# Rotary embedding, interleaved: how the last three batch rows leave the chip

## The chip, the cores and the metric

The kernel runs on one core of one Trainium2 chip. The metric is the device time of one execution in microseconds. A profile of one execution, taken by the hardware profiler, stands beside the times; its times count from the start of its span.

## What is computed

The input `x` has shape (8, 2048, 16, 64) in fp32: batch, sequence position, head, head dimension. Neighbouring elements of the head dimension form pairs, and each pair is rotated by an angle that depends on the position and the pair; `cos` and `sin` have shape (2048, 32).

```python
x_pairs = x.reshape(batch, seq_len, num_heads, head_dim // 2, 2)
x1 = x_pairs[..., 0]
x2 = x_pairs[..., 1]
out1 = x1 * cos - x2 * sin
out2 = x1 * sin + x2 * cos
out = np.stack([out1, out2], axis=-1).reshape(batch, seq_len, num_heads, head_dim)
```

The output has the shape and the type of `x`. So 67.1 MB are read and 67.1 MB written in HBM, and each element takes three arithmetic operations.

## The kernel before

The 2048 positions are laid over 128 partitions with K = 16 positions each. One batch row (called a row below) is thus a tile of 128 partitions by 16 x 1024 elements, 8.39 MB in fp32. In SBUF a row is held in bf16. The tile `xt` has NX = 5 places for rows, and the list `HOME` gives each row its place: rows 5, 6 and 7 use the places of rows 0, 1 and 2 again.

The conversion between fp32 in HBM and bf16 in SBUF is done by the DMA itself. Such a casting DMA is issued by GpSimd: `load(b, n)` and `store(b, n)` (lines 61 to 67) move n rows each with one DMA, and all of them are in one queue, GpSimd's. There are two exceptions, at the two ends of the kernel. The first four positions of row 0 (HEAD) come in as fp32 by a DMA that SyncE issues, into the tile `st`, and ScalarE casts them (line 101). The last four positions of row 7 (TAIL) go out by the same way backwards: ScalarE casts them to fp32 (line 132), and SyncE issues the DMA (line 133).

`rotate(b)` (lines 69 to 88) is three VectorE instructions over a row: a product with the sine table into the scratch tile `qt`, a product with the cosine table in place, and a sum in place that reads `qt` with the two elements of each pair exchanged.

The order is written out by hand, under a manual schedule. GpSimd works its instructions off in that order; each waits for the semaphores of what it needs. The loads of rows 0 to 4 are all issued at the start. Behind them GpSimd's order is:

```python
store(0, 1)
store(1, 2)                 # behind rotate(2)
load(5, 1)
load(6, 2)
store(3, 2)                 # behind rotate(4)
store(5, 2)                 # behind rotate(6)
# line 127: row 7 without its last four positions, behind rotate(7)
```

Then the tail follows. Line 131 is a ScalarE copy of one element into the place of row 6, and so it waits for the store of rows 5 and 6 to have landed. The cast of line 132 and the DMA of line 133 stand behind it.

The kernel ends with a closing sequence, which the profile puts on line 159: SyncE waits for the DMAs, each engine drains, and the engines meet by semaphores.

Of the kernel before, what the change touches and what calls it, by code (L numbers as in the profile page):

```python
# [2 lines left out]

# [4 lines left out]


@with_exitstack  # L10
def kernel(
    ctx: ExitStack,
    tc: tile.TileContext,
    x: bass.AP,
    cos: bass.AP,
    sin: bass.AP,
    out: bass.AP,
):
    nc = tc.nc
    fp32 = mybir.dt.float32  # L20
    bf16 = mybir.dt.bfloat16
    mult = mybir.AluOpType.mult
    add = mybir.AluOpType.add

    B, S, H, D = x.shape
    P = 128
    K = S // P
    KP = 16
    D2 = D // 2
    HD = H * D  # L30
    NX = 5
    HEAD = 4
    TAIL = 4
    LAST = 2


    HOME = [0, 1, 2, 3, 4, 0, 1, 2]

    x_t = x.rearrange("b (p k) h d -> b p k (h d)", p=P, k=K)
    out_t = out.rearrange("b (p k) h d -> b p k (h d)", p=P, k=K)  # L40
    x_r = x.rearrange("b (p k) h d -> p b (k h d)", p=P, k=K)
    out_r = out.rearrange("b (p k) h d -> p b (k h d)", p=P, k=K)
    cos_t = cos.rearrange("(p k) c -> p (k c)", p=P, k=K)
    sin_t = sin.rearrange("(p k) c -> p (k c)", p=P, k=K)

    consts = ctx.enter_context(tc.tile_pool(name="consts", bufs=1))
    stage = ctx.enter_context(tc.tile_pool(name="stage", bufs=1))

    xt = consts.tile([P, NX, K * HD], bf16)
    cos_sb = consts.tile([P, K * D2], fp32)  # L50
    sin_sb = consts.tile([P, K * D2], fp32)
    c_tab = consts.tile([P, K, D], bf16)
    s_tab = consts.tile([P, K, D], bf16)

    gate = consts.tile([1, 1], bf16)
    mark = consts.tile([1, 1], bf16)

    def home(b, k0=0, k1=K):
        return xt[:, HOME[b], k0 * HD : k1 * HD].rearrange("p (k c) -> p k c", c=HD)

    def load(b, n):
        h = HOME[b]
        nc.gpsimd.dma_start(out=xt[:, h : h + n], in_=x_r[:, b : b + n])  # L63

    def store(b, n):
        h = HOME[b]
        nc.gpsimd.dma_start(out=out_r[:, b : b + n], in_=xt[:, h : h + n])  # L67

    def rotate(b, k0=0, k1=K):
        nk = k1 - k0  # L70
        xp = home(b, k0, k1)
        qt = stage.tile([P, KP, HD], bf16, name="qt", tag="work")

        def rows(a):
            return a.rearrange("p k (h e) -> p k h e", h=H, e=D)

        def tab(a):
            return dataclasses.replace(
                a, offset=a.offset + k0 * D, ap=[a.ap[0], [D, nk], [0, H], [1, D]]
            )  # L80

        nc.vector.tensor_tensor(out=rows(qt[:, :nk]), in0=rows(xp), in1=tab(s_tab), op=mult)  # L82
        nc.vector.tensor_tensor(out=rows(xp), in0=rows(xp), in1=tab(c_tab), op=mult)  # L83
        q_swap = dataclasses.replace(
            qt, offset=qt.offset + 1, ap=[qt.ap[0], [2, nk * HD // 2], [-1, 2]]
        )
        x3 = xp.rearrange("p k (a j) -> p (k a) j", j=2)
        nc.vector.tensor_tensor(out=x3, in0=x3, in1=q_swap, op=add)  # L88

    with tc.manual_schedule():  # L90
        head = stage.tile([P, TAIL, HD], fp32, name="st", tag="work")
        nc.sync.dma_start(out=head[:, :HEAD], in_=x_t[0, :, :HEAD])
        nc.gpsimd.dma_start(out=home(0, HEAD), in_=x_t[0, :, HEAD:])  # L93
        nc.gpsimd.dma_start(out=cos_sb, in_=cos_t)  # L94
        nc.gpsimd.dma_start(out=sin_sb, in_=sin_t)  # L95
        load(1, 2)
        load(3, 1)
        nc.gpsimd.dma_start(out=home(4, 0, K - LAST), in_=x_t[4, :, : K - LAST])  # L98
        nc.gpsimd.dma_start(out=home(4, K - LAST), in_=x_t[4, :, K - LAST :])  # L99

        nc.scalar.copy(out=home(0, 0, HEAD), in_=head[:, :HEAD])  # L101
        s2 = s_tab.rearrange("p k (i j) -> p (k i) j", j=2)
        nc.vector.tensor_copy(out=s2[:, :, 0], in_=sin_sb)  # L103
        nc.vector.tensor_scalar_mul(s2[:, :, 1], sin_sb, -1.0)  # L104
        nc.vector.tensor_copy(  # L105
            out=c_tab.rearrange("p k (i j) -> p (k i) j", j=2),
            in_=cos_sb.to_broadcast([P, K * D2, 2]),
        )
        rotate(0, 0, HEAD)
        rotate(0, HEAD, K)  # L110
        nc.scalar.copy(out=gate, in_=home(4, K - LAST - 1, K - LAST)[:1, 0, :1])  # L111
        nc.scalar.copy(out=xt[:1, HOME[0], :1], in_=xt[:1, HOME[0], :1])  # L112
        store(0, 1)
        rotate(1)
        rotate(2)
        nc.gpsimd.tensor_copy(out=mark, in_=xt[:1, 4, K * HD - 1 :])  # L116
        store(1, 2)
        load(5, 1)
        load(6, 2)
        rotate(3)  # L120
        rotate(4)
        store(3, 2)
        for b in range(5, B):
            rotate(b)
            if b == 6:
                store(5, 2)
        nc.gpsimd.dma_start(out=out_t[B - 1, :, : K - TAIL], in_=home(B - 1, 0, K - TAIL))  # L127

        tail = stage.tile([P, TAIL, HD], fp32, name="st", tag="work")
        last = home(B - 1, K - TAIL, K)  # L130
        nc.scalar.copy(out=xt[:1, HOME[B - 2], :1], in_=xt[:1, HOME[B - 1], K * HD - 1 :])  # L131
        nc.scalar.copy(out=tail, in_=last)  # L132
        nc.sync.dma_start(out=out_t[B - 1, :, K - TAIL :], in_=tail)


# [1 line left out]
_INS = ['x', 'cos', 'sin']  # L137
_OUTS = [((8, 2048, 16, 64), 'float32')]


# [23 lines left out]
```

## Time and profile before

| what | value |
|---|---|
| median of 3 runs | 316.26 us (316.24 to 316.33) |
| span of the profiled execution | 314.4 us; the profile gives no total of its own for it, so the runs stand beside it, 1.8 to 1.9 us above |
| VectorE busy | 210.4 us (67%) |
| ScalarE busy | 8.9 us (3%) |
| GpSimd busy | 13.9 us (4%) |
| GpSimd's DMA queue | 98.04 MB, 96.8% of 16 engines |
| SyncE's DMA queue | 4.19 MB, 3.3% of 16 engines |
| HBM | 67.63 MB read, 67.11 MB written |

DVE is VectorE, ACT ScalarE, POOL GpSimd, SP SyncE; a "q" behind the name is the engine's queue or sequencer. An instruction that issues a DMA is not counted as busy time of the transfer: it is done after half a microsecond or so, while the data move much later. For each DMA issue the profile gives the time to its landing, which is when the completion of the whole transfer has been signalled. The size in KB that stands beside some issues is that of the destination.

### The profile page before, as it was taken

To read this page: it belongs to the slowest core of one execution; us is meant where nothing else is said; L and a number is where in the kernel's file an instruction comes from. 1 tells how busy PE (TensorE), PEld (TensorE's weight loads), DVE (VectorE), ACT (ScalarE), POOL (GpSimd) and SP (SyncE) were. 2 spreads that over 40 slices of the span, in tenths; PEclk is the share of its full clock that TensorE was granted. 3 is DMA by queue.
4 is the path that set the end of the run, shared out by engine and by line. 5 is a ranking of instruction groups with operands and counts; after the bars stand their busy time and mean duration, and the time that the engine had idled before them with its cause. 6 is when DMAs were issued, how large, how long until landed. Compare 5 with 4: busy or idle time off the path is not lost.

```text
span 314.4 us, 116 instructions
## 1 busy us (share of the span) xinstructions
DVE 210.4 (67%) x30; ACT 8.9 (3%) x6; POOL 13.9 (4%) x19
## 2 busy tenths in 40 slices
DVE  0009995099999999999992399903999999200000
ACT  1040000000000000000000000000000000000400
POOL 5000000000002400000000000000000000000000
DMA  7999999999999999999999999999999999999997
GB/s 254 263 283 200 200 200 267 200 200 213 229 233 258 425 509 400 400 459 475 400 200 246 221 200 200 254 213 333 400 525 409 400 400 525 409 400 400 434 434 333
DMA packets 2816, 102.24 MB, mean 325 GB/s; under 512 B 256, under 2 KB 256, under 8 KB 512
## 3 DMA queue, kind: packets, MB, share of 16 engines
q0 software_dynamic: 2528, 98.04, 96.8%
q1 hardware_dynamic: 288, 4.19, 3.3%
HBM read 67.63 MB, written 67.11 MB: 429 GB/s over the span
## 4 chain that ended last, share of the span: by engine, by line
another core or an unknown queue 87%; DMA 5%; ACT 1%; ACTq 1%; issue 0%
DMA st<-in_x_dram 5%; ACT xt L101 1%; ACTq L159 1%; ACT xt L131 0%; ACT xt L112 0%; ACTq L131 0%; ACT gate L111 0%
## 5 line engine op out<-in xcount | busy, mean ns | idle before, releaser
L82 DVE TENSOR_TENSOR qt<-xt,s_tab 128x16384 bf16<-128x16384 bf16 (+2 forms) x9 | 69.7, 7743 | 34.4 <-DMA xt<-in_x_dram 34.3
L83 DVE TENSOR_TENSOR xt<-xt,c_tab 128x16384 bf16<-128x16384 bf16 (+2 forms) x9 | 69.7, 7744 | 0.4
L88 DVE TENSOR_TENSOR xt<-xt,qt 128x16384 bf16<-128x16384 bf16 (+2 forms) x9 | 69.7, 7744 | 0.3
L103 DVE CAST s_tab<-sin_sb 128x512 bf16<-128x512 f32 x1 | 0.5, 458 | 23.8 <-DMA sin_sb<-in_sin_dram 23.8
L67 POOL DMA_DIRECT2D out_dram<-xt x4 | 2.7, 671 | 185.5 <-ACT xt L112 93.8
L131 ACT COPY xt<-xt 1x1 bf16<-1x1 bf16 x1 | 0.2, 193 | 195.4 <-DMA out_dram<-xt 195.4
L116 POOL COPY mark<-xt 1x1 bf16<-1x1 bf16 x1 | 5.0, 5014 | 1.4 <-DMA xt<-in_x_dram 1.4
L63 POOL DMA_DIRECT2D xt<-in_x_dram x4 | 2.6, 656 | 43.0 <-DMA out_dram<-xt 43.0
L101 ACT CAST xt<-st 128x4096 bf16<-128x4096 f32 x1 | 3.6, 3604 | 13.3 <-DMA st<-in_x_dram 13.3
L132 ACT CAST st<-xt 128x4096 f32<-128x4096 bf16 x1 | 3.6, 3598 | 0.0
L111 ACT COPY gate<-xt 1x1 bf16<-1x1 bf16 x1 | 0.2, 193 | 79.7 <-DMA xt<-in_x_dram 79.7
L127 POOL DMA_DIRECT2D out_dram<-xt x1 | 0.6, 572 | 25.5 <-DVE xt L88 25.5
L101 ACT ACT_TABLE_LOAD x1 | 1.3, 1283 | 0.7 <-PEq L148 0.7
L93 POOL DMA_DIRECT2D xt<-in_x_dram x1 | 0.7, 680 | 0.8 <-PEq L159 0.8
L105 DVE CAST c_tab<-cos_sb 128x1024 bf16<-128x1024 f32 x1 | 0.7, 684 | 0.0
L99 POOL DMA_DIRECT2D xt<-in_x_dram x1 | 0.6, 592 | 0.0
L98 POOL DMA_DIRECT2D xt<-in_x_dram x1 | 0.6, 586 | 0.0
L95 POOL DMA_DIRECT2D sin_sb<-in_sin_dram x1 | 0.6, 562 | 0.0
L94 POOL DMA_DIRECT2D cos_sb<-in_cos_dram x1 | 0.6, 554 | 0.0
L104 DVE TENSOR_SCALAR s_tab<-sin_sb 128x512 bf16<-128x512 f32 x1 | 0.4, 445 | 0.0
L112 ACT COPY xt<-xt 1x1 bf16<-1x1 bf16 x1 | 0.2, 189 | 0.0
L148 POOL MEMSET const-float32-0.0<- 128x1 f32 x1 | 0.1, 93 | 0.2 <-issue 0.2
(3 smaller groups left out, 0.3 us busy)
## 6 DMA issues: line engine op xcount, KB each, us to landing
xt<-in_x_dram POOLq DMA_DIRECT2D x2, 8192.0 KB, 58.5
xt<-in_x_dram POOLq DMA_DIRECT2D x2, 4096.0 KB, 67.6
out_dram<-xt POOLq DMA_DIRECT2D x1, 6144.0 KB, 40.9
xt<-in_x_dram POOLq DMA_DIRECT2D x1, 3584.0 KB, 94.3
xt<-in_x_dram POOLq DMA_DIRECT2D x1, 3072.0 KB, 21.2
st<-in_x_dram SPq DMA_DIRECT2D x1, 2048.0 KB, 14.5
out_dram<-st SPq DMA_DIRECT2D x1, 2048.0 KB, 15.5
xt<-in_x_dram POOLq DMA_DIRECT2D x1, 512.0 KB, 96.3
```

The costliest lines, as they stand in the source:

```text
L63: nc.gpsimd.dma_start(out=xt[:, h : h + n], in_=x_r[:, b : b + n])
L67: nc.gpsimd.dma_start(out=out_r[:, b : b + n], in_=xt[:, h : h + n])
L82: nc.vector.tensor_tensor(out=rows(qt[:, :nk]), in0=rows(xp), in1=tab(s_tab), op=mult)
L83: nc.vector.tensor_tensor(out=rows(xp), in0=rows(xp), in1=tab(c_tab), op=mult)
L88: nc.vector.tensor_tensor(out=x3, in0=x3, in1=q_swap, op=add)
L93: nc.gpsimd.dma_start(out=home(0, HEAD), in_=x_t[0, :, HEAD:])
L94: nc.gpsimd.dma_start(out=cos_sb, in_=cos_t)
L101: nc.scalar.copy(out=home(0, 0, HEAD), in_=head[:, :HEAD])
L105: nc.vector.tensor_copy(out=c_tab.rearrange("p k (i j) -> p (k i) j", j=2), in_=cos_sb.to_broadcast([P, K * D2, 2]),)
L116: nc.gpsimd.tensor_copy(out=mark, in_=xt[:1, 4, K * HD - 1 :])
L132: nc.scalar.copy(out=tail, in_=last)
L159: with _tile.TileContext(nc) as tc:
```

## The change

The store of rows 5 and 6 is split, and its second half is joined with row 7. Row 5 is stored alone, behind rotate(5). Rows 6 and 7 leave in one casting DMA of GpSimd, behind rotate(7). The fp32 tail with its two ScalarE copies and its DMA on SyncE is gone; `TAIL` is gone, and the tile `head` takes its size from `HEAD`, which is the same number. In the changed kernel the lines up to the change stand one line higher. In its compiled order VectorE's instructions are the same; ScalarE has two less, SyncE one DMA less, and GpSimd as many as before: its last two are the store of row 5, which waits for row 5's load and for VectorE, and the store of rows 6 and 7, which waits for their load and for VectorE.

```diff
     HEAD = 4
-    TAIL = 4
     LAST = 2
...
-        head = stage.tile([P, TAIL, HD], fp32, name="st", tag="work")
+        head = stage.tile([P, HEAD, HD], fp32, name="st", tag="work")
...
         store(3, 2)
-        for b in range(5, B):
-            rotate(b)
-            if b == 6:
-                store(5, 2)
-        nc.gpsimd.dma_start(out=out_t[B - 1, :, : K - TAIL], in_=home(B - 1, 0, K - TAIL))
-
-        tail = stage.tile([P, TAIL, HD], fp32, name="st", tag="work")
-        last = home(B - 1, K - TAIL, K)
-        nc.scalar.copy(out=xt[:1, HOME[B - 2], :1], in_=xt[:1, HOME[B - 1], K * HD - 1 :])
-        nc.scalar.copy(out=tail, in_=last)
-        nc.sync.dma_start(out=out_t[B - 1, :, K - TAIL :], in_=tail)
+        rotate(5)
+        store(5, 1)
+        rotate(6)
+        rotate(7)
+        store(6, 2)
```

## The prediction

> **What bounds the kernel now.** I read the page first: its strip of 40 slices, then the DMA queue's view over a few narrow stretches of time to get the landing of single transfers, then the instructions of the closing line and the waits of SyncE.
>
> The page's strip. Each digit is the busy share of one fortieth of the span in tenths; DMA is the mean of the 16 DMA engines.
>
> ```profile
> span 314.4 us, 116 instructions
> DVE 210.4 (67%) x30; ACT 8.9 (3%) x6; POOL 13.9 (4%) x19
> DVE  0009995099999999999992399903999999200000
> ACT  1040000000000000000000000000000000000400
> DMA  7999999999999999999999999999999999999997
> HBM read 67.63 MB, written 67.11 MB: 429 GB/s over the span
> ```
>
> The DMA engines are full from the first slice to the last; VectorE, the only engine with real work, is 67% busy and finishes 45 us before the end. The kernel is a stream of bytes over one full pipe. Only three things can move the time: the bytes, a hole in the stream, or what stands before its first and behind its last byte.
>
> The DMA queue's view, asked over stretches that hold one issue each. The last column is the time from issue to landing: the first three are the stores of batch row 0 (stretch 99 to 100), of rows 3 and 4 (167 to 168) and of rows 5 and 6 (243 to 244); the last two are row 7 in its two pieces.
>
> ```profile
> out_dram<-xt POOLq DMA_DIRECT2D x1, 21.3
> out_dram<-xt POOLq DMA_DIRECT2D x1, 88.1
> out_dram<-xt POOLq DMA_DIRECT2D x1, 50.8
> out_dram<-xt POOLq DMA_DIRECT2D x1, 6144.0 KB, 40.9
> out_dram<-st SPq DMA_DIRECT2D x1, 2048.0 KB, 15.5
> ```
>
> And the timeline of the last issues and of what precedes them (start, duration, engine, line):
>
> ```profile
> 195.87 8.69 DVE L88 TENSOR_TENSOR xt<-xt,qt 128x16384 bf16<-128x16384 bf16 x1
> 243.46 0.70 POOL L67 DMA_DIRECT2D out_dram<-xt  x1 [75.19 <-DVE xt L88]
> 260.64 8.69 DVE L88 TENSOR_TENSOR xt<-xt,qt 128x16384 bf16<-128x16384 bf16 x1
> 269.63 0.57 POOL L127 DMA_DIRECT2D out_dram<-xt  x1 [25.46 <-DVE xt L88]
> 298.05 0.35 SPq L133 DMA_DIRECT2D out_dram<-st  x1
> ```
>
> Adding the two: rows 3 and 4 (issued at 167.55) land at 255.65, rows 5 and 6 at 294.26, the bf16 piece of row 7 at 310.53, its fp32 tail at 313.55. Rows 5 and 6 took 38.6 us of a full pipe, 19.3 us for one batch row of 8.39 MB; row 7 in two pieces on two queues took 313.55 - 294.26 = 19.3 us too. So a cast row and a row that is part cast, part plain fp32 cost the same.
>
> The third view is that of the closing line: its instructions by engine, with shortest, median and longest duration in ns, and first and last start.
>
> ```profile
> L159 POOLq EVENT_SEMAPHORE  x4: 17/17/17, 313.7 to 314.3; - x4
> L159 POOLq DRAIN  x3: 45/87/41561, 269.6 to 314.2; - x3
> L159 SPq DRAIN  x3: 7/7/7, 313.7 to 314.0; - x3
> ```
>
> The fourth is the waits of SyncE (who waited for what, us in total, times, longest):
>
> ```profile
> SPq L159 <- DMA out_dram<-xt: 12.1, 1, 12.1
> SPq L159 <- DMA out_dram<-st: 2.8, 1, 2.8
> ```
>
> GpSimd starts a DRAIN at 269.6, as soon as its last DMA (row 7's bf16 piece) is issued, and stays in it 41.56 us, to 311.17: 0.64 us longer than the landing of that DMA at 310.53. (The longest must be the one that starts first: a later one of that length would run past the span.) SyncE waits 12.1 us for the bf16 piece and then 2.8 us more, alone, for the fp32 tail. At 313.7, about 0.2 us behind the tail's landing, GpSimd meets the others with its first closing semaphore, and the closing sequence runs 0.7 us to the end at 314.4. GpSimd's DRAIN was over 2.5 us before that, so it cost nothing.
>
> **The change part by part.** The sum is made against the profiled span of 314.4 us; the runs have a median of 316.26, so some 1.9 us lie around the span, and I keep them.
>
> *Bytes and pieces.* HBM traffic stays: the tail wrote 2.1 MB of fp32 from fp32, and now the same 2.1 MB are written from bf16. Three stores behind that of rows 3 and 4 become two. Expected landing of the last byte: 255.65 + 3 x 19.3 = 313.55, the same as before. One boundary between DMAs is lost. Its price is bounded by row 0's store, which followed a load on the same queue: the load (row 4's last piece, issued at 4.78, 96.3 us to landing) landed at 101.08, the store at 99.19 + 21.3 = 120.49, so 19.4 against 19.3: at most 0.1 us. I take 0, the value that is nearest to the tail itself: row 7 in two DMAs took no longer than half of rows 5 and 6 in one.
>
> *Row 5's store moves forward*, from 243.46 (behind rotate(6)) to about 204.9, when rotate(5) ends (195.87 + 8.69 = 204.56) and 0.3 us for the semaphore. GpSimd has nothing behind it until the last store, so its wait holds nobody up. The queue is still busy: rotate(6) starts at 217.01, when the load of rows 6 and 7 has landed, then come rows 3 and 4 until 255.65, then row 5 until 274.95. It starts no earlier than the first half of today's double store: value 0, covered by 51 us of queue. Nothing waits for these landings but the end.
>
> *The last store* is issued where L127 is now, at 269.63, since it needs rotate(7). It must be ready when row 5 drains at 274.95: a margin of 5.3 us. The nearest row for the time from issue to data is row 0's store: issued at 99.19, it ran behind a load that landed at 101.08 with no hole, so descriptors take at most 1.9 us. (One issue of two rows holds GpSimd 0.70 us, of one 0.57.) Cost 0, with 3.4 us of cover; beyond that each microsecond is lost in full. Before, the backlog at this point reached to 294.26, so the change spends 19.3 us of cover and leaves 5.3.
>
> *Taken away*: two ScalarE copies (0.19 and 3.60 us at 294.3) and SyncE's issue, which lay beside 16 us of row 7's bf16 piece. Value 0.
>
> A rule that would price this differently is in the Trainium skill, "DMA: Bandwidth & Descriptors", section on the anatomy of one DMA: each GpSimd DMA costs a fixed 2.0 us or so beside its bytes. By that page's figure, an estimate, one DMA fewer would save about 2 us if the fixed part were serial; the 19.4 us behind a boundary do not show it in this stream.
>
> *The end.* This is the step with a price. Today the last DMA to land belongs to SyncE, and GpSimd's DRAIN ends 2.4 us earlier. After the change the last to land is GpSimd's own, so the 0.64 us by which its DRAIN outlasts its last landing come behind the last byte: GpSimd meets the others at 313.55 + 0.64 = 314.2, not at 313.7. SyncE's own closing (0.2 us behind the landing, and some semaphores of 28 ns) lies beside it. That is 0.64 - 0.2, some +0.45 us; the 0.7 us behind are unchanged. Bounds: 0 if the DRAIN is not tied to the landing, and from below -0.1 (the boundary); above, the delay may grow with what the last DMA moves: it has 256 row pieces against 128 (2 x 0.64 = 1.28, +1.09 us) and 16.8 MB against 6.3 (2.7 x 0.64 = 1.71, +1.5 us). I take 0.64, the one measured.
>
> Sum: 0 (bytes) + 0 (row 5 early) + 0 (margin) + 0 (ScalarE) + 0.45 = 0.45: span 314.85, time 316.26 + 0.45 = 316.7.
>
> **The rivals.**
> 1. *Nothing moves.* GpSimd's DRAIN ends at 311.17 for another reason, or the delay overlaps SyncE's closing. For it: there is only one such DRAIN in the trace. Against: nothing else that the views show ends at 311.2, and the DRAIN lasted through 41 us in which GpSimd had no other instruction. Time 316.2 to 316.35. Chance 0.17.
> 2. *The DRAIN's tail grows with the last DMA* (slower). Place: GpSimd between the last landing and its meeting with the others. It decides from a delay of about 0.82 us, where the loss passes 0.63 us. By row pieces 316.26 + 1.09 = 317.35, by bytes 317.8. For it: a drain that clears up after its transfer would take longer for more pieces, and issuing two rows does take longer than one (0.70 against 0.57), but far from twice. Chance 0.17.
> 3. *A hole before the last store.* If data follow the issue only after more than 5.3 us, or row 5 drains sooner, the pipe stands idle from 274.95. At 8 us from issue to data it would be +2.7, 319.0. Against it: the bound of 1.9 us. Chance 0.04.
> 4. *Faster.* Each DMA carries a fixed part that the stream waits for, and there is one DMA fewer. The most that the rows leave for it is the 1.9 us from row 0's issue to the landing ahead of it: 316.7 - 1.9 = 314.8. Against it: the two landings 19.4 us apart, which leave 0.1. The fixed cost of the Trainium skill's page, above, is this rival's rule. Chance 0.04.
>
> **How the numbers follow.** The forecast case, a DRAIN delay of some 0.4 to 0.8 us on the path, has 0.58; its own range is 316.45 to 316.85. The range reaches from rival 1 to rival 2 by row pieces: 316.2 to 317.35; left out are rivals 3 and 4 and rival 2 by bytes. A measurement of this kernel can tell about 0.2% from no change, 0.63 us. Within it: the forecast and rival 1, 0.58 + 0.17 = 0.75 (the forecast would need a delay over 0.82 us to leave it, which is rival 2). Slower by more: rivals 2 and 3, 0.21. Faster by more: rival 4, 0.04.
>
> **What the changed profile would show.** Right: the last store issued near 269.6 and landing near 313.5; 19.3 us per row with no slice of the strip below 9 between 255 and 313; GpSimd's long DRAIN ending about 0.6 us behind the last landing, its first closing semaphore near 314.2 where it was 313.7; span 314.85. Wrong: a landing later than 313.7 (hole or slower rows), a DRAIN that ends with SyncE's wait (rival 1), or one that outlasts the landing by over 0.8 us (rival 2).

## The result, and the profile after

The changed kernel takes 316.76 us (median of 17 runs) where the kernel before took 316.26 (also 17 runs): a ratio of 1.0019, with a 95% interval of 1.0012 to 1.0026. (The ratio and its interval are made from all the runs, so it is not quite the ratio of the two medians; this holds for the experiments too.) It is slower by half a microsecond. That is inside the 0.63 us, 0.2%, that the prediction set as the bound of "the same", though the interval reaches a little beyond it. The forecast was 316.7. The profiled execution took 316.65 us, with a span of 314.9 against 314.4.

The page of the changed kernel:

```profile
span 314.9 us, 113 instructions
DVE  0009995099999999999992399904999999200000
ACT  1030000000000000000000000000000000000000
DMA  7999999999999999999999999999999999999996
HBM read 67.63 MB, written 67.11 MB: 428 GB/s over the span
```

The bytes are the same, and the DMA strip has no gap where the stores of row 5 and of rows 6 and 7 meet; only its last digit fell, from 7 to 6, in a slice that reaches from 307 us to past the last landing. The time is behind the last byte, not in the stream.

The timeline of the two stores, and the DMA queue's view of the same two issues (us to landing):

```profile
204.89 0.55 POOL L66 DMA_DIRECT2D out_dram<-xt  x1 [36.62 <-DVE xt L87]
269.66 0.70 POOL L66 DMA_DIRECT2D out_dram<-xt  x1 [64.22 <-DVE xt L87]
```

```profile
out_dram<-xt POOLq DMA_DIRECT2D x1, 70.1
out_dram<-xt POOLq DMA_DIRECT2D x1, 43.9
```

Row 5 lands at 274.99, rows 6 and 7 at 313.56. The last landing was 313.55 before.

The closing line, which is line 152 in this kernel (shortest, median, longest duration in ns, first and last start):

```profile
L152 POOLq EVENT_SEMAPHORE  x4: 17/17/17, 314.2 to 314.8; - x4
L152 POOLq DRAIN  x3: 45/82/44530, 269.6 to 314.6; - x3
L152 SPq DRAIN  x3: 7/7/7, 313.8 to 314.4; - x3
```

SyncE reaches its first DRAIN at 313.8, 0.2 us behind the landing. GpSimd's long DRAIN runs from 269.6 for 44.53 us, to 314.2, and its first closing semaphore follows at once. In the kernel before that semaphore came at 313.7. So the whole difference of the spans lies between the last landing and GpSimd's arrival.

### The profile page after: what moved, and what is told of

It reads as the page before. It is cut to its first block, busy times and chain, and to the rows that moved or that the text cites. A ratio compares the mean times of both kernels' runs of the same rounds, so it can differ in the third digit from the quotient of the medians.

```text
span 314.9 us, 113 instructions
## 1 busy us (share of the span) xinstructions
DVE 210.3 (67%) x30; ACT 5.2 (2%) x4; POOL 13.8 (4%) x19
## 4 chain that ended last, share of the span: by engine, by line
DVE 50%; issue 17%; another core or an unknown queue 11%; POOLq 0%; POOL 0%; DVEq 0%
DVE xt L82 17%; DVE xt L87 17%; DVE qt L81 17%; POOLq L152 0%; DVE c_tab L104 0%; POOL out_dram L66 0%; DVEq L81 0%; DVEq L82 0%; POOLq L66 0%
## 6 DMA issues: line engine op xcount, KB each, us to landing
xt<-in_x_dram POOLq DMA_DIRECT2D x1, 3072.0 KB, 21.3
cos_sb<-in_cos_dram POOLq DMA_DIRECT2D x1, 256.0 KB, 21.3
```

## The experiments

The theory, called the drain theory below, is the one of the prediction: GpSimd's closing DRAIN outlasts GpSimd's own last landing by about 0.6 us, and this costs time only when no other landing comes later. Its rivals were that the fp32 tail is the cheaper way to move the last bytes, that the early store of row 5 or the thin margin behind it costs, that each DMA has a fixed price in the stream, and that the DRAIN's tail grows with the last DMA. Two things are called tail here: the fp32 tail is the last four positions of row 7, and the DRAIN's tail is the time by which GpSimd's long DRAIN outlasts the last landing of GpSimd's DMAs.

**The order of landings alone.** The kernel before, without the copy that holds the tail back:

```diff
-        nc.scalar.copy(out=xt[:1, HOME[B - 2], :1], in_=xt[:1, HOME[B - 1], K * HD - 1 :])
```

> The kernel before without the one-element copy that holds the fp32 tail back, so the tail's cast follows rotate(7) directly and SyncE issues its DMA near 273 instead of 298. Same bytes, same pieces, fp32 tail still on SyncE; only the order of the last landings changes. Drain theory (GpSimd's DRAIN outlasts its own last landing by about 0.6 us and costs only when that landing is the last): the tail lands some 7 us early, GpSimd's bf16 piece lands last near 313.55, DRAIN ends near 314.17, first closing semaphore near 314.2, span 314.85, time 316.7. Rival (the fp32 tail over SyncE is itself the cheaper way to move the last bytes): span 314.4, time 316.3.

Measured: 317.01 us against 316.29, ratio 1.0020 (1.0011 to 1.0029). From its DMA queue's view and its closing line:

```profile
out_dram<-xt POOLq DMA_DIRECT2D x1, 6144.0 KB, 44.1
out_dram<-st SPq DMA_DIRECT2D x1, 2048.0 KB, 40.6
```

```profile
L158 POOLq EVENT_SEMAPHORE  x4: 17/17/17, 314.6 to 315.1; - x4
L158 POOLq DRAIN  x3: 45/95/44784, 269.7 to 315.0; - x3
```

The fp32 tail is there, on SyncE, and the kernel is as slow as the changed one or slower. GpSimd's piece, issued at 269.75, now lands last, at 313.9, and the DRAIN runs on to 314.5. That turns down the rival of the cheaper fp32 tail. Two sizes were off. The last landing is 0.3 us later than in the kernels before and after, which accounts for the rest of the 0.7 us. Some 0.1 us of that is there long before the end (row 0's store is issued at 99.31, where it was 99.19 before); what makes the rest was not settled. And the tail, issued at 273.12, landed at 313.7, not 7 us early but 0.2: it shared the pipe to the end.

**Each half of the change alone.** First the tail's removal, with rows 5 and 6 still together:

```diff
-        nc.gpsimd.dma_start(out=out_t[B - 1, :, : K - TAIL], in_=home(B - 1, 0, K - TAIL))
...
-        nc.sync.dma_start(out=out_t[B - 1, :, K - TAIL :], in_=tail)
+        store(7, 1)
```

> The kernel before with row 7 stored whole by one GpSimd DMA, rows 5 and 6 still together behind rotate(6): the removal of the fp32 tail alone, no early store of row 5. Drain theory: 316.7, DRAIN 0.6 us behind the landing. Rival (row 5's store issued early, or the thin margin of 5.3 us at the last store, is what costs): 316.3. Rival (the DRAIN's tail grows with the pieces of the last DMA, 128 here and 256 in the changed kernel): DRAIN delay near 0.3 us, 316.4.

Then the split, with the tail as it was:

```diff
-            if b == 6:
-                store(5, 2)
+            if b < 7:
+                store(b, 1)
```

> The kernel before with rows 5 and 6 stored by a DMA each, behind rotate(5) and rotate(6), tail as before over SyncE: one GpSimd DMA more and the early store alone. Drain theory: SyncE lands last, 316.3, span 314.4, with at most 0.1 us for one more boundary. Rival (early store of row 5 costs): 316.7. A fixed part of 2 us for each DMA: 318.3.

Measured: without the tail 316.66 us, ratio 1.0012 (1.0003 to 1.0020); with the split alone 316.29, ratio 1.0000 (0.9991 to 1.0009), each against 316.29. From the closing line without the tail:

```profile
L153 POOLq EVENT_SEMAPHORE  x4: 17/17/17, 314.2 to 314.8; - x4
L153 POOLq DRAIN  x3: 45/82/44507, 269.7 to 314.6; - x3
```

GpSimd's first closing semaphore comes at 314.2, as in the changed kernel. So the early store of row 5 costs nothing that these runs can tell (the interval is 0.3 us to either side), and the removed tail costs as much as the whole change. The DRAIN outlasted a last DMA of 128 row pieces by the same 0.62 us as one of 256.

**More DMAs in the stream.** The changed kernel with its last store in four, and with row 6 alone and row 7 in eight:

```diff
-        store(6, 2)
+        for b, k in ((6, 0), (6, 8), (7, 0), (7, 8)):
+            nc.gpsimd.dma_start(out=out_t[b, :, k : k + 8], in_=home(b, k, k + 8))
```

> The changed kernel with rows 6 and 7 stored by four GpSimd DMAs of half a row each instead of one, all behind rotate(7): three boundaries more, last DMA 4.2 MB. Boundaries at 0 to 0.1 us each: 316.7 to 317.0. Fixed part of 2 us for each DMA: 322.8. DRAIN delay 0.6 us if it does not depend on the last DMA's size, 0.3 or less if it does.

(The two halves of row 6 were issued at 243.42, since they wait for rotate(6) only; the expectation had all four behind rotate(7).)

```diff
-        store(6, 2)
+        store(6, 1)
+        for k in range(0, K, 2):
+            nc.gpsimd.dma_start(out=out_t[7, :, k : k + 2], in_=home(7, k, k + 2))
```

> The changed kernel with row 6 stored alone and row 7 by eight GpSimd DMAs of two positions each (piece size 8 KB per partition): ten DMAs behind that of rows 3 and 4 instead of two, the last ones held back until an earlier DMA has landed, since eight semaphores go round. Boundaries: 8 more at 0 to 0.05 us (four_pieces showed its landing unmoved) give 0 to 0.4 us. DRAIN delay 0.6 us if it is fixed for a DRAIN; 0.9 or more if it grows by the 0.04 us for each DMA that four_pieces may have shown. Time 316.7 to 317.4. A fixed part of 2 us for each DMA would give 332.7.

Measured: 316.89 us, ratio 1.0019 (1.0011 to 1.0028), and 317.29, ratio 1.0026 (1.0015 to 1.0036), both against 316.29. The last of the ten DMAs was issued at 294.52. Its DRAIN, and its time to landing from the DMA queue's view:

```profile
L154 POOLq DRAIN  x3: 45/90/20254, 294.5 to 315.2; - x3
```

```profile
out_dram<-xt POOLq DMA_DIRECT2D x1, 1024.0 KB, 19.3
```

The landing, 313.82, is 0.26 us later than in the changed kernel, so eight boundaries more cost about 0.03 us each. The DRAIN lasts 20.25 us, 0.95 longer than the transfer. Its tail did not shrink with a last DMA of 1 MB: it grew, and there are more DMAs.

**A hole, and how much cover is enough.** Rows 5 to 7 in one DMA, behind rotate(7); and the kernel before with a tail of one position:

```diff
         rotate(5)
-        store(5, 1)
         rotate(6)
         rotate(7)
-        store(6, 2)
+        store(5, 3)
```

> The changed kernel with rows 5, 6 and 7 in one GpSimd DMA behind rotate(7): no early store of row 5, so the queue runs dry when rows 3 and 4 have left (255.65) and the price of a hole and the time from issue to data show. Issue at 269.66; if data follow after 1.0 to 1.9 us (the bound of the prediction), they begin near 271 in place of 255.2, the last byte lands near 329.0 to 330, time 332.2 to 333.1. If the time from issue to data were above 5.3 us, the last landing would be beyond 333 and the changed kernel would have had a hole too. DRAIN delay 0.6 us if it does not depend on the pieces (384 here, 256 in the changed kernel), 0.9 if it does.

```diff
-    TAIL = 4
+    TAIL = 1
```

> The kernel before with a tail of one position in place of four (0.5 MB of fp32 over SyncE). Estimate from the windows of before: the small pieces of the tail alternate with the last pieces of the bf16 part, about half of them remain at the end, so SyncE lands some 0.5 us behind GpSimd. Drain theory: the end is the later of SyncE's landing + 0.2 and GpSimd's landing + 0.65, so 0.45 us of cover is enough: 316.3, as before. If cover takes the four positions: 316.5 to 316.7.

Measured: 332.51 us, ratio 1.0513 (1.0496 to 1.0531), and 316.33, ratio 0.9998 (0.9989 to 1.0007), both against 316.29. The windows of the first, around the issue at 269.58 (length, busy time of VectorE, ScalarE and GpSimd, clock, share of the DMA engines, GB/s):

```profile
257.00:269.00 12.00, 11.97 (x2) 0.00 (x0) 0.00 (x0) 1.00 0.00 0
269.00:270.00 1.00, 0.28 (x1) 0.00 (x0) 0.42 (x1) 1.00 0.00 0
270.00:271.00 1.00, 0.00 (x0) 0.00 (x0) 0.33 (x1) 1.00 1.98 852
```

(A transfer counts whole in the window where it starts, so a share can pass 1.) The pipe stands empty until the issue, and data flow within 1.4 us of it. The DMA lands 59.7 us after its issue, 1.8 more than three rows of 19.3. So the last store of the changed kernel had about 3.5 us of its 5.3 to spare. With a tail of one position the records of the trace have SyncE's landing last by only 0.44 us (313.55 against 313.11). From its closing line:

```profile
L159 POOLq EVENT_SEMAPHORE  x4: 17/17/17, 313.8 to 314.4; - x4
L159 POOLq DRAIN  x3: 45/87/44117, 269.6 to 314.2; - x3
L159 SPq DRAIN  x3: 7/7/7, 313.6 to 314.0; - x3
```

The DRAIN ends at 313.73, and GpSimd's first closing semaphore follows at 313.77, some 0.05 us after SyncE is ready. So 0.44 us covers the DRAIN almost to its end, and the time shows no loss.

**What the DRAIN's tail grows with.** Two more runs put GpSimd's DMAs elsewhere than at the end:

```diff
-        load(3, 1)
+        for k in range(0, K, 4):
+            nc.gpsimd.dma_start(out=home(3, k, k + 4), in_=x_t[3, :, k : k + 4])
...
-        store(3, 2)
+        for b, k in ((3, 0), (3, 8), (4, 0), (4, 8)):
+            nc.gpsimd.dma_start(out=out_t[b, :, k : k + 8], in_=home(b, k, k + 8))
```

> The changed kernel with row 3 loaded by four GpSimd DMAs and rows 3 and 4 stored by four: six GpSimd DMAs more (20 in place of 14), all landed well before the DRAIN begins at 269.6; the last two stores are as in the changed kernel. So far the way from the last landing to GpSimd's first closing semaphore was 0.61 us with 13 GpSimd DMAs in the kernel (three_rows), 0.65 with 14, 0.76 with 17 (four_pieces), 0.97 with 22 (ten_dmas). Theory A, the DRAIN's tail grows by 0.041 us with every GpSimd DMA of the whole kernel: 0.65 + 6 x 0.041 = 0.89, time 316.67 + 0.25 = 316.9. Theory B, it grows with the DMAs that are still open when the DRAIN begins: 0.65, time 316.7.

```diff
-        nc.gpsimd.dma_start(out=cos_sb, in_=cos_t)
-        nc.gpsimd.dma_start(out=sin_sb, in_=sin_t)
+        nc.sync.dma_start(out=cos_sb, in_=cos_t)
+        nc.sync.dma_start(out=sin_sb, in_=sin_t)
```

> The changed kernel with the two tables loaded by SyncE in place of GpSimd: 12 GpSimd DMAs in place of 14, none of them at the end. Theory A: 0.65 - 2 x 0.041 = 0.57 us from the last landing to GpSimd's closing semaphore, time 316.6 if the start is as before. Theory B: 0.65, 316.7.

Measured: 317.21 us, ratio 1.0031 (1.0019 to 1.0042), and 334.08, ratio 1.0560 (1.0545 to 1.0574), both against 316.24. In the first the last store was issued at 269.77, and by the DMA queue's view and the closing line

```profile
out_dram<-xt POOLq DMA_DIRECT2D x1, 44.0
```

```profile
L154 POOLq DRAIN  x3: 45/82/44884, 269.8 to 315.1; - x3
```

the DRAIN lasts 0.88 us longer than the transfer, though all six DMAs more had landed before it began. The records of the trace, which have the end of the DRAIN and the last signal of GpSimd's DMAs to the nanosecond, give one line through all kernels:

| GpSimd DMAs in the kernel | kernel | DRAIN behind the last landing, us |
|---|---|---|
| 12 | tables over SyncE (fewer_dmas) | 0.537 |
| 13 | three rows at once (three_rows) | 0.578 |
| 14 | before, the changed kernel (both profiles), tail_early, join_only, tail_one | 0.618 to 0.619 |
| 15 | split_only | 0.660 |
| 17 | four_pieces | 0.741 |
| 20 | more_early_dmas | 0.863 |
| 22 | ten_dmas | 0.945 |

That is 0.041 us for each DMA that GpSimd issued in the whole kernel and 0.05 us besides ((0.945 - 0.537) / 10 = 0.041; 0.537 - 12 x 0.041 = 0.05). Neither the size of the last DMA nor what was open when the DRAIN began fits: more_early_dmas ends exactly as the changed kernel does. Nor does the number of row pieces: three_rows and the changed kernel, and likewise split_only and the kernel before, move the same pieces and differ by one DMA alone. The time of more_early_dmas passed the expectation of 316.9 by 0.3 us; 0.2 us of that is its last landing, 313.77, which was later as well, and the rest is open.

The time of the last run missed its expectation by 17 us, for another reason. The DMA strip of its page (span 332.3 us), its timeline, and its DMA queue's view of the two tables:

```profile
DMA  9999999898999920599898989889898989889895
```

```profile
55.52 0.46 DVE L102 CAST s_tab<-sin_sb 128x512 bf16<-128x512 f32 x1 [55.52 <-DMA sin_sb<-in_sin_dram]
```

```profile
cos_sb<-in_cos_dram SPq DMA_DIRECT2D x1, 256.0 KB, 31.6
sin_sb<-in_sin_dram SPq DMA_DIRECT2D x1, 256.0 KB, 53.9
```

The tables of 0.26 MB each needed 31.6 and 53.9 us over SyncE, where the sine table had landed at 23.8 in GpSimd's order. VectorE began 32 us late, and from about 121 to 137 us the DMA engines stood empty, because the next rows to be stored were not yet rotated. For the DRAIN's tail the run still counts: it has 12 DMAs, and the tail is 0.537 us.

**The changed kernel once more,** in a later set of runs:

> The changed kernel once more beside the kernel before on this chip, to see how far its time spreads: 316.7; a DRAIN delay that varies from run to run would show as times from 316.5 to 317.5, a fixed one as a spread no wider than that of before.

Measured: 316.67 us against 316.29, ratio 1.0010 (1.0001 to 1.0019), with eleven runs between 316.58 and 316.81. The times up to 317.8 of the first set did not come back, while the kernel before had times up to 317.21 here; what makes the longer times is open. In both profiles of the changed kernel the DRAIN's tail is 0.62 us.

No run beat the kernel before: its DRAIN is covered already, and the stream is full.

## Why the prediction was right

*Bytes and pieces.* The last landing was set at 313.55 and came at 313.56. The boundary, 0 to 0.1 us, came out at about 0.03 in ten_dmas. The fixed 2.0 us for each GpSimd DMA that the Trainium skill states ("DMA: Bandwidth & Descriptors", the anatomy of one DMA) would have added 16 us in ten_dmas; the landing moved by 0.26, so in this full queue it does not add up. The prediction's estimate of some 2 us saved had a slip besides: that price is for GpSimd's DMAs, of which both kernels issue 14, and the DMA that the change takes away is SyncE's.

*Row 5's store.* It was issued at 204.89 (204.9 forecast) and landed at 274.99 (274.95). Alone, it made no difference to the median (split_only).

*The last store's margin.* Descriptors were bounded at 1.9 us; three_rows shows 1.8 in landings and 1.4 to the first data. There was no hole.

*The end.* The DRAIN's tail was taken at 0.64 us, worked out from a landing to a tenth of a microsecond, and is 0.62 in the records; the meeting was forecast near 314.2 and came at 314.2; the span forecast of 314.85 stands against 314.9. The time rose by 0.50 us in the first set of runs and by 0.38 in the later one, where 0.45 was forecast.

*Rivals.* The first, that nothing moves, fell with the changed profile (first closing semaphore at 314.2 where it was 313.7) and with join_only. The second, that the tail grows with the last DMA, was wrong in what it named: 128, 256 and 384 pieces gave 0.62, 0.62 and 0.58 us. The tail does grow, but with the number of GpSimd's DMAs, and that number is 14 in both kernels. The one measured value could be carried over because of that. The prediction did not know it and took 0.64 only as the one value it had, so in this step the size was right by luck, while the mechanism, a DRAIN that outlasts the last landing, was right as argued. The third and fourth, a hole and a fixed cost for each DMA, did not occur.

## What to carry to other kernels

When a kernel streams without a hole, look at who lands last: what still follows behind that landing is the end of the kernel. Here, with GpSimd's DMA last, the closing DRAIN added 0.4 to 0.5 us to the end, and a small transfer by SyncE that landed half a microsecond later covered it; one position of sixteen was enough with 14 GpSimd DMAs. Look for such a tail in the long DRAIN of the closing line, even where it is covered and costs nothing yet, and count GpSimd's DMAs.

## What the runs showed of the hardware

GpSimd's DRAIN lasts until the last DMA of its queue has landed, and then 0.05 us and 0.041 us for every DMA that GpSimd has issued since the start, whatever their sizes and however long ago they landed (12 to 22 DMAs, 0.537 to 0.945 us in these runs). What it does in that time no profile shows.

A small transfer on a second queue was not done early beside a deep first one: two tables of 0.26 MB needed 31.6 and 53.9 us over SyncE beside GpSimd's loads (fewer_dmas; 21.2 and 21.3 us in GpSimd's own order before), and the tail of tail_early, 2.1 MB, needed 40.6 us.
